# Moving first-table tiles, adaLN units and unsplit products between the stages of a two-layer step

## The chip, the cores and the metric

One core of a Trainium2 chip runs the whole step as one program. The time is device microseconds from the start to the end of one execution, the median of several; smaller is better. PE (TensorE) does the matmuls and PEld its weight loads, DVE (VectorE) and ACT (ScalarE) work on elements, POOL (GpSimd) issues the gathers, SP and ACT issue the plain DMAs.

## What is computed

Two layers, each over 128 prompt tokens and 512 latent tokens of width 1024. A layer has an adaLN part (shift, scale and gate vectors, a product of a condition with `w_ada`), four mixer branches, an output product, and at the end the expert part, which is what the change touches:

```
def peer(u, lp):                       # xt: 512 latent tokens x 1024
    q = (xt @ lp['w_peer_q']).reshape(t, 8, 2, 128)
    sc = einsum('thpc,hpkc->thpk', q, lp['peer_keys'])     # 8 heads, 2 halves, 128 keys
    v1, i1 = top_k(sc[:, :, 0], 16); v2, i2 = top_k(sc[:, :, 1], 16)
    cand = v1[..., :, None] + v2[..., None, :]
    cidx = i1[..., :, None] * 128 + i2[..., None, :]
    top, pos = top_k(cand, 16)
    idx = take_along_axis(cidx, pos); w = softmax(top)
    act = gelu(einsum('td,tkd->tk', xb, tab_u[ib]))        # 16384 experts of width 1024
    out = einsum('tk,tkd->td', wb * act, tab_v[ib])
```

The adaLN part is `m = silu(cond) @ w_ada + b_ada`, cut into six vectors; the second layer norm of a layer uses two of them, and the residual after the experts uses the gate `g2`.

## The kernel before, in words

The prompt tokens run as a generator of small steps (`hook` takes a few at a time at a low priority, by rates that differ from stage to stage); the latent tokens are the main line. Of the 512 latent tokens one block of 128 fetches its expert rows one by one (`gather`, L1207: indirect DMAs on POOL, dot products and sums on DVE). The other three blocks, 384 tokens, are taken densely against all 16384 experts, 128 tiles of 128 experts. A framework orders the instructions of each engine when the program is built: what is ready in its own model of time and stands first in the source goes first. The engines then run their lists in order.

A float32 product is made in one of two ways. *Split*: `load_unit` (L338) loads 512 KB, ACT casts it to a high part (`whi`), DVE subtracts to get a low part (`wlo`), and PE makes three products for each of 8 blocks, 24 matmuls. *Unsplit*: `load_raw` (L333) alone, and PE makes 8 float32 products (16 instructions in the trace). The pool `wp` holds three raw tiles and three pairs of parts.

The expert part of a layer goes through these stages:

- `ln_mod` (L488) makes the normalized, modulated tokens `u` (two parts) and `raw` (one float32 tile in the buffer `big`), and the first two of the 16 query products.
- *The selection*, `peer_top` (L1079): for each of the 16 half heads a query product (`gemm_T`, L346, split, or `gemm_raw`, L358, unsplit where `g % 4 < PQF[l]`), and scores against the keys (L1087). After the second half of a head come `select` (DVE: top 16 of each half, of the candidates, and the indices) and `AQ[l]` adaLN units. One unit (`ada_unit`, L405) loads 2 x 512 KB and makes 8 small matmuls and a few more.
- *Early tiles*, `s_early` (L1250): layer 1 only, `NEA = (0, 4)`. Four tiles of the first table are made unsplit from `raw`, and their gelu is written to DRAM (`gsp`); they are tiles 6, 36, 66 and 96.
- *The weight build*, `wdense` (L1120): the selected weights become a dense matrix W, 12 groups of 32 tokens. DVE and ACT make one-hot tiles, PE multiplies them (L1172), ACT copies 2 MB for each group, and SP writes them to DRAM (`wst`). After each group come `AW[l]` adaLN units.
- *The start*: the adaLN units that are left, a transpose for the gather, and tiles 0 to 5 of the first table (`s_stage`, L1267, split: 24 matmuls, a gelu, kept in `gel`, which has 8 buffers; all use one bank of PSUM, `psS`).
- *The loop*: for each of 128 tiles the columns of W are read back (every fourth tile, `big<-wst`), tile j+6 of the first table is made or, if stored, read (`s_load`), the gelu of tile j is multiplied by W (`v_stage`, L1279) and tile j of the second table is multiplied into the sums (`v_mm`, L1289: 18 matmuls, line 1292). Rows of the gather and steps of the prompt run beside it.

In layer 0 the queue of adaLN units holds 24 when the selection begins (20 for layer 1, 4 for the last gate of layer 0): 8 are called for in the selection, 12 in the weight build, 4 after it. In layer 1 it holds 4, called for in the first groups of the weight build.

Of the kernel before, what the change touches and what calls it, by code (L numbers as in the profile page):

```python
# [8 lines left out]
F32 = mybir.dt.float32  # L9
# [36 lines left out]
GLAG = (6, 1)  # L46
PLAG = (4, 2)
PGL = 0
PQF = (0, 2)
SCB = 6  # L50
LND = 2
NLN = (0, 0)
NPP = 1
WPAD = 128
FILL = (2, 6)
AQ = (1, 0)
AW = (1, 1)
NEA = (0, 4)
LT = 3
NAO = (1, 1)  # L60
AUTO = 2
# [172 lines left out]
def build(tc, A, O, layers=L, tap=None, stop=None):  # L234
# [35 lines left out]
    def P2(name="p2"):  # L270
        return pss.tile([128, 1024], F32, name=name, tag="s")
# [61 lines left out]
    def load_raw(src, op=None):  # L333
        raw = (op or wp).tile([128, 1024], F32, name="wraw", tag="wraw", bufs=8 if op else None)
        nc.sync.dma_start(raw, src)
        return raw
# [110 lines left out]
    def ada_step(n=1, rp=None):  # L447
        for _ in range(max(min(n, len(pend) - hold[0]), 0)):
            ada_unit(*pend.pop(0), rp)
# [626 lines left out]
        V.reciprocal(sm, sm)  # L1076
        tt(out, ex, sm[:, :, None].to_broadcast([128, n, 16]), ALU.mult)

    def peer_top(l, u, pre, raw, scg, idx, wsel, tp):  # L1079
        tops = tp.tile([128, ND, 8, 16], F32, name="topsd", tag="topsd")  # L1080
        with tc.tile_pool(name=f"pq{l}", bufs=2) as qp:
            scs = []

            def score(hd, p, qc, ky):
                pk = P1()
                for b in range(NS):
                    PE.matmul(pk[:, b * 128:(b + 1) * 128], qc[:, b * 128:(b + 1) * 128], ky, start=True, stop=True)  # L1087
                sc = qp.tile([128, ND, 128], F32, name="sc", tag="sc", bufs=SCB)
                S.copy(sc.rearrange("p a b -> p (a b)"), pk[:, 128:T])
                S.copy(scg[:, p, hd], pk[:, 0:128])  # L1090
                scs.append(sc)
                if p:
                    s2 = scs[-2:]
                    for _ in select(tp, ND, lambda p: (lambda b: s2[p][:, b]), idx[:, :, hd], tops[:, :, hd]):
                        pass
                    ada_step(AQ[l])

            last = None
            for g in range(16):
                ky = qp.tile([128, 128], F32, name="ky", tag="ky", bufs=3)  # L1100
                nc.scalar.dma_start(ky, A["keys"][l, :, g * 128:(g + 1) * 128])
                ps = pre[g] if g < 2 else P1()
                if g < 2:
                    pass
                elif g % 4 < PQF[l]:
                    gemm_raw(ps, A["w_pq"][l, g], raw)
                else:
                    gemm_T(ps, load_unit(A["w_pq"][l, g]), u)
                qc = qp.tile([128, T], F32, name="qc", tag="qc")
                S.copy(qc, ps)  # L1110
                if last:
                    score(*last)
                last = (g // 2, g % 2, qc, ky)
                if g == 1:
                    score(*last)
                    last = None
            score(*last)
        topsoft(tp, wsel.rearrange("p a h k -> p (a h) k"), tops.rearrange("p a h k -> p (a h) k"), ND * 8)

    def wdense(l, idx, wsel, wst, wb):  # L1120
        f = lambda a: a.rearrange("p a b -> p (a b)")
        iotam = wb.tile([128, 128, TI], F16, name="iotam", tag="iotam")
        S.copy(iotam, cst[:, C_IOTA:C_IOTA + 128][:, :, None].to_broadcast([128, 128, TI]))
# [22 lines left out]
        for g in range(TD // TW):  # L1146
# [28 lines left out]
                hook(0.5)  # L1175
            nc.sync.dma_start(wst[:, g, :128 * TW], stg.rearrange("p a b -> p (a b)"))
            ada_step(AW[l])

    def rows_of(src, rows, use, gp, bufs, lags):
        q = []  # L1180
# [66 lines left out]
            for _ in nxt:  # L1247
                pass

    def s_early(l, i, raw, sps, dp):  # L1250
        w = load_raw(A["peer_ut"][l, early(l, i)])
        ps = sps[:, i % 2 * 512:i % 2 * 512 + TD]
        for k in range(KD):
            PE.matmul(ps, w[:, k * 128:(k + 1) * 128], raw[:, k, 128:T], start=(k == 0), stop=(k == KD - 1))
        ge = dp.tile([128, TD], F32, name="gel", tag="gel", bufs=NGEL)
        act(ge, ps, AF.Gelu)
        nc.sync.dma_start(gsp[l][i], ge)

    def early(l, i):
        return NGEL - 2 + i * ((128 - NGEL + 2) // max(NEA[l], 1))  # L1260

    def s_load(l, i, dp):
        ge = dp.tile([128, TD], F32, name="gel", tag="gel", bufs=NGEL)
# [31 lines left out]
    def peer(l, u, pre, raw, acc):  # L1295
# [3 lines left out]
        scg = tp.tile([128, 2, 8, 128], F32, name="scg")  # L1299
        idx = tp.tile([128, ND, 8, 16], I32, name="idx")  # L1300
        wsel = tp.tile([128, ND, 8, 16], F32, name="wsel")
        peer_top(l, u, pre, raw, scg, idx, wsel, tp)
        if NEA[l]:
            sps = P2("psS")
            for i in range(NEA[l]):
                s_early(l, i, raw, sps, dp)
        at = {early(l, i): i for i in range(NEA[l])}
        sps = PP("psS") if NPP > 1 else P1("psS")
        with tc.tile_pool(name=f"wb{l}", bufs=1) as wb:
            wdense(l, idx, wsel, wsts[l], wb)  # L1310
        ada_step(len(pend))
        gp = pool(f"pg{l}", 1, fst)
        sh = big()
# [4 lines left out]
                PE.matmul(pt[:, k * 128:(k + 1) * 128], fp(ublk(u[i], k, 0)), ident, start=(i == 0), stop=(i == 1))  # L1318
        S.copy(xts, pt)
        del pt  # L1320
        gels = {j: s_stage(l, j, u, sps, dp) for j in range(NGEL - 2)}
        rate[:] = R_P[l]
        gen = gather(l, scg, xts, acc, tp, gp)
        outs = []
# [574 lines left out]

    dram = pool("dram", 1, space=bass.MemoryType.DRAM)  # L1900
    wsts = [dram.tile([128, TD // TW, 128 * TW + WPAD], F32, name=f"wst{l}") for l in range(layers)]
    gsp = [[dram.tile([128, TD], F32, name=f"gs{l}_{i}") for i in range(NEA[l])] for l in range(layers)]
    x1ds = [[dram.tile([128, D], F32, name=f"x1d{l}_{b}") for b in range(NS)] for l in range(layers)]
    px1 = [dram.tile([128, D], F32, name=f"px1_{l}") for l in range(layers)]
    xins = [[A["x"][(b + 1) * 128:(b + 2) * 128, :] for b in range(NS)]]
# [48 lines left out]
```

## Time and profile before

| | us |
|---|---|
| median of 3 runs | 4409.49 (4405.4 to 4415.57) |
| the profiled execution | 4427.92 |
| its span, first to last instruction | 4426.0 |
| PE busy | 4162.7 |
| DVE busy | 3470.6 |
| ACT busy | 1784.9 |

The profiled execution is one of its own and 18.4 us above the median. Stages of it, in us from the start of the span: layer 0 has its selection from 881 to 1043, its weight build to 1158 and its loop from 1209 on; layer 1 has them from 3071, to 3221, to 3342, and the loop from 3360 to the end. A busy PE is not a PE at its peak: neighbouring matmuls overlap in the records. How long a product takes is therefore read from the chain of waits or from a group's busy time, not from the mean of one matmul.

### The profile page before, as it was taken

What the parts mean: (1) busy time and instruction counts of PE and PEld (TensorE: products, weight loads), DVE (VectorE), ACT (ScalarE), POOL (GpSimd) and SP (SyncE); (2) the same over time, 40 slices, a digit from 0 to 9 for tenths busy, and PEclk for the clock granted to TensorE, in tenths of its full rate; (3) what the DMA queues carried; (4) which work ended last, traced back from release to release, by engine and by line L of the source; (5) the groups of instructions that cost most, each with busy time, mean ns of one, the idle gap of its engine ahead of it and who ended that gap; (6) DMA issues with size and microseconds to landing.
All of it is one profiled execution on the core that took longest, in us unless ns stands there. A gap on an engine that the chain in (4) does not pass through costs nothing.

```text
span 4426.0 us, 63067 instructions
## 1 busy us (share of the span) xinstructions
PE 4162.7 (94%) x22534; PEld 3444.5 (78%) x22534; DVE 3470.6 (78%) x7189; ACT 1784.9 (40%) x3134; POOL 1367.5 (31%) x1028
## 2 busy tenths in 40 slices
PE   8999999787799999999998999998888999999998
PEld 5677677664599999898987667777557889889897
DVE  2236888799998888777777688777999988788887
ACT  3234343347643333433335343433485333333333
POOL 0000443100254444244440044230003554455541
PEclk8999999898899999999999999998989999999999
DMA  6654676537899999899995577473268999999996
GB/s 225 207 189 150 226 236 218 173 126 251 313 358 340 347 337 335 275 359 336 345 342 187 183 243 240 162 240 135 85 238 328 356 346 331 336 334 349 358 333 214
DMA packets 440857, 1182.41 MB, mean 267 GB/s; under 512 B 43056, under 2 KB 153696, under 8 KB 437216
## 3 DMA queue, kind: packets, MB, share of 16 engines
q1 hardware_dynamic: 279600, 625.72, 41.0%
q0 software_dynamic: 147456, 536.94, 34.2%
q10 hardware_dynamic: 13488, 15.75, 1.1%
q8 instruction: 177, 2.90, 0.3%
q14 instruction: 136, 1.11, 0.1%
HBM read 1116.05 MB, written 62.19 MB: 266 GB/s over the span
## 4 chain that ended last, share of the span: by engine, by line
PE 72%; DVE 12%; DMA 8%; issue 4%; ACT 3%; POOL 1%; ACTq 0%; SPq 0%; POOLq 0%; DVEq 0%
PE psS L1273 22%; PE pout L1292 21%; PE p L352 9%; PE pp L1446 5%; DVE eq L246 1%; POOL row L1188 1%; PE pss L646 1%; DVE wlo L246 1%; DMA wraw<-in_peer_v_dram 1%; PE pss L641 1%; PE psw L1172 1%; PE p L681 1%; PE psada L420 1%; DMA row<-in_peer_u_dram,pidx 1%; PE p L511 1%
## 5 line engine op out<-in xcount | busy, mean ns | idle before, releaser
L341 ACT CAST whi<-wraw 128x1024 fp32r<-128x1024 f32 x662 | 694.5, 1050 | 1024.1 <-PE psS L1273 645.1
L246 DVE TENSOR_TENSOR wlo<-wraw,whi 128x1024 fp32r<-128x1024 f32 x662 | 806.8, 1220 | 360.2 <-ACT whi L341 357.8
L1273 PE MATMUL psS<-u,whi 128*128 128x384 f32 x4032 | 1052.5, 342 | 33.6 <-ACT gel L243 27.8
L1273 PEld LDWEIGHTS psS<-u,whi 128*128 128x128 f32 x4032 | 742.1, 190 | 61.8 <-ACT gel L243 34.1
L1273 PE MATMUL psS<-u,wlo 128*128 128x384 f32 x2016 | 687.4, 341 | 4.9 <-DVE wlo L246 4.9
L1188 POOL DMA_INDIRECT row<-in_peer_u_dram,pidx x256 | 317.5, 1240 | 1187.2 <-ACT pidx L1067 460.8
L352 PE MATMUL p<-u,whi 128*128 128x512 f32 (+1 forms) x1760 | 596.0, 414 | 5.6 <-ACT whi L341 5.2
L1188 POOL DMA_INDIRECT row<-in_peer_u_dram,idg x256 | 359.7, 1405 | 616.2 <-DVE dots L1199 383.8
L1188 POOL DMA_INDIRECT row<-in_peer_v_dram,idg x256 | 363.8, 1421 | 533.7 <-DVE accs L1205 446.2
L1188 POOL DMA_INDIRECT row<-in_peer_v_dram,pidx x256 | 326.3, 1275 | 654.8 <-DVE pacc L1205 283.1
L1292 PE MATMUL pout<-wlo,ph 128*128 128x512 f32 x1536 | 502.1, 402 | 0.0
L1292 PE MATMUL pout<-whi,ph 128*128 128x512 f32 x1536 | 500.5, 401 | 1.0 <-ACT whi L341 1.0
L1292 PE MATMUL pout<-whi,pl 128*128 128x512 f32 x1536 | 500.1, 401 | 0.0
L352 PEld LDWEIGHTS p<-u,whi 128*128 128x128 f32 (+1 forms) x1760 | 328.9, 191 | 89.6 <-issue 10.6
L1273 PEld LDWEIGHTS psS<-u,wlo 128*128 128x128 f32 x2016 | 383.0, 190 | 6.0 <-DVE wlo L246 5.7
L352 PE MATMUL p<-u,wlo 128*128 128x512 f32 (+1 forms) x880 | 362.2, 412 | 19.3 <-DVE wlo L246 19.1
L1205 DVE SCALAR_TENSOR_TENSOR pacc<-row,pdots,pacc 128x1024 f32<-128x1024 f32 x254 | 324.8, 1279 | 35.7 <-PE p L352 25.9
L1199 DVE CUSTOM_DVE_ANT_0 row<-row,pu 128x1024 f32<-128x1024 f32 x256 | 310.4, 1218 | 49.8 <-DMA row<-in_peer_u_dram,pidx 26.1
L1284 ACT CAST ph<-gel 128x384 fp32r<-128x384 f32 x256 | 131.3, 513 | 528.1 <-PE pout L1292 510.5
L1292 PEld LDWEIGHTS pout<-whi,pl 128*128 128x128 f32 x1536 | 287.6, 188 | 64.5 <-issue 0.8
L1292 PEld LDWEIGHTS pout<-wlo,ph 128*128 128x128 f32 x1536 | 287.0, 188 | 62.8 <-issue 0.6
L1205 DVE SCALAR_TENSOR_TENSOR accs<-row,ge,accs 128x1024 f32<-128x1024 f32 x254 | 325.7, 1282 | 5.6
(494 smaller groups left out, 6564.0 us busy)
## 6 DMA issues: line engine op xcount, KB each, us to landing
wraw<-in_peer_ut_dram SPq DMA_DIRECT2D x256, 512.0 KB
wraw<-in_peer_v_dram SPq DMA_DIRECT2D x256, 512.0 KB
wraw<-in_w_ada_dram SPq DMA_DIRECT2D x96, 512.0 KB
wraw<-in_w_in_dram SPq DMA_DIRECT2D x96, 512.0 KB
pw<-in_w_in_dram SPq DMA_DIRECT2D x192, 256.0 KB
big<-wst SPq DMA_DIRECT2D x64, 768.0 KB
wst<-stg SPq DMA_DIRECT2D x12, 2048.0 KB
wst<-big SPq DMA_DIRECT2D x12, 2048.0 KB
```

Of the source, the lines that this page charges most:

```text
L246: V.tensor_tensor(out=out, in0=a, in1=b, op=op)
L341: S.copy(hi, raw)
L352: i = PE.matmul(ps[:m, :T], a[:, o:o + m], b[:, k], start=(n == 0), stop=(n == 3 * KD - 1))
L420: PE.matmul(ps[32 * k:32 * k + 32, :256], c32[:, 4 * hf + k, :], w[:, k * 256:(k + 1) * 256], start=(hf == 0), stop=(hf == 1 and not (isg ...
L511: i = PE.matmul(p, a[:, k * 128:(k + 1) * 128], b[:, k], start=(k + n == 0), stop=(k == KD - 1 and n == 2))
L1188: pace(G.indirect_dma_start(out=t, out_offset=None, in_=A[src], in_offset=bass.IndirectOffsetOnAxis(ap=ix, axis=0)), lags[0])
L1199: return V.tensor_tensor_reduce(out=t, in0=t, in1=x, scale=1.0, scalar=0.0, op0=ALU.mult, op1=ALU.add, accum_out=dst)
L1205: return V.scalar_tensor_tensor(out=acc, in0=t, scalar=ge, in1=acc, op0=ALU.mult, op1=ALU.add)
L1273: PE.matmul(ps, a[:, k * 128:(k + 1) * 128], b[:, k, 128:T], start=(n == 0), stop=(n == 3 * KD - 1))
L1284: S.copy(ph, ge)
L1292: PE.matmul(outs[d][hf], a[:, d * 128:(d + 1) * 128], b[:, hf * 512:(hf + 1) * 512], start=(j == 0 and i == 0), stop=(j == 127 and i == le ...
L1446: i = PE.matmul(ps[:m, :128], w[k // 4][:, o:o + m], u[:, k], start=(k == 0), stop=(k == KD - 1))
```

## The change

- `s_early` is replaced by `s_raw` and a generator `raw_tiles`. Both layers make 6 unsplit tiles (`NRAW = (6, 6)`; tiles 6, 26, 46, 66, 86 and 106), one after the `select` of each head from the second on, instead of none in layer 0 and four after the selection in layer 1. They use a bank of the pool of single banks.
- `split_tiles` yields once after each group of the weight build: nothing six times, then tiles 0 to 5 of the first table, one after each of the last six groups. Before, they came after the build. `NSPL` is (0, 0), so no split tile is stored.
- `PQF` goes from (0, 2) to (2, 2): in layer 0 six of the 14 query products of the selection become unsplit, as they are in layer 1.
- adaLN units: `NLN` goes from (0, 0) to (4, 4), four units ahead of `ln_mod`; `AQ` from (1, 0) to (0, 0), none in the selection; `AW` from (1, 1) to (2, 1), two after each group of layer 0's build.

```diff
--- before.py
+++ after.py
@@ -46,16 +46,17 @@
 GLAG = (6, 1)
 PLAG = (4, 2)
 PGL = 0
-PQF = (0, 2)
+PQF = (2, 2)
 SCB = 6
 LND = 2
-NLN = (0, 0)
+NLN = (4, 4)
 NPP = 1
 WPAD = 128
 FILL = (2, 6)
-AQ = (1, 0)
-AW = (1, 1)
-NEA = (0, 4)
+AQ = (0, 0)
+AW = (2, 1)
+NRAW = (6, 6)
+NSPL = (0, 0)
 LT = 3
 NAO = (1, 1)
 AUTO = 2
@@ -1076,7 +1077,7 @@
         V.reciprocal(sm, sm)
         tt(out, ex, sm[:, :, None].to_broadcast([128, n, 16]), ALU.mult)
 
-    def peer_top(l, u, pre, raw, scg, idx, wsel, tp):
+    def peer_top(l, u, pre, raw, scg, idx, wsel, tp, early):
         tops = tp.tile([128, ND, 8, 16], F32, name="topsd", tag="topsd")
         with tc.tile_pool(name=f"pq{l}", bufs=2) as qp:
             scs = []
@@ -1094,6 +1095,8 @@
                     for _ in select(tp, ND, lambda p: (lambda b: s2[p][:, b]), idx[:, :, hd], tops[:, :, hd]):
                         pass
                     ada_step(AQ[l])
+                    if hd:
+                        next(early, None)
 
             last = None
             for g in range(16):
@@ -1117,7 +1120,7 @@
             score(*last)
         topsoft(tp, wsel.rearrange("p a h k -> p (a h) k"), tops.rearrange("p a h k -> p (a h) k"), ND * 8)
 
-    def wdense(l, idx, wsel, wst, wb):
+    def wdense(l, idx, wsel, wst, wb, early):
         f = lambda a: a.rearrange("p a b -> p (a b)")
         iotam = wb.tile([128, 128, TI], F16, name="iotam", tag="iotam")
         S.copy(iotam, cst[:, C_IOTA:C_IOTA + 128][:, :, None].to_broadcast([128, 128, TI]))
@@ -1175,6 +1178,7 @@
                 hook(0.5)
             nc.sync.dma_start(wst[:, g, :128 * TW], stg.rearrange("p a b -> p (a b)"))
             ada_step(AW[l])
+            next(early, None)
 
     def rows_of(src, rows, use, gp, bufs, lags):
         q = []
@@ -1247,17 +1251,34 @@
             for _ in nxt:
                 pass
 
-    def s_early(l, i, raw, sps, dp):
-        w = load_raw(A["peer_ut"][l, early(l, i)])
-        ps = sps[:, i % 2 * 512:i % 2 * 512 + TD]
+    def early_at(l):
+        n = NRAW[l] + NSPL[l]
+        return [NGEL - 2 + i * ((128 - NGEL + 2) // n) for i in range(n)]
+
+    def s_raw(l, j, raw, dp):
+        w = load_raw(A["peer_ut"][l, j])
+        ps = P1("psS")[:, :TD]
         for k in range(KD):
             PE.matmul(ps, w[:, k * 128:(k + 1) * 128], raw[:, k, 128:T], start=(k == 0), stop=(k == KD - 1))
         ge = dp.tile([128, TD], F32, name="gel", tag="gel", bufs=NGEL)
         act(ge, ps, AF.Gelu)
-        nc.sync.dma_start(gsp[l][i], ge)
-
-    def early(l, i):
-        return NGEL - 2 + i * ((128 - NGEL + 2) // max(NEA[l], 1))
+        return ge
+
+    def raw_tiles(l, raw, dp):
+        for i in range(NRAW[l]):
+            nc.sync.dma_start(gsp[l][i], s_raw(l, early_at(l)[i], raw, dp))
+            yield
+
+    def split_tiles(l, u, sps, dp, gels):
+        n = TD // TW - NSPL[l] - (NGEL - 2)
+        for _ in range(n):
+            yield
+        for i in range(NRAW[l], NRAW[l] + NSPL[l]):
+            nc.sync.dma_start(gsp[l][i], s_stage(l, early_at(l)[i], u, sps, dp))
+            yield
+        for j in range(NGEL - 2):
+            gels[j] = s_stage(l, j, u, sps, dp)
+            yield
 
     def s_load(l, i, dp):
         ge = dp.tile([128, TD], F32, name="gel", tag="gel", bufs=NGEL)
@@ -1299,15 +1320,18 @@
         scg = tp.tile([128, 2, 8, 128], F32, name="scg")
         idx = tp.tile([128, ND, 8, 16], I32, name="idx")
         wsel = tp.tile([128, ND, 8, 16], F32, name="wsel")
-        peer_top(l, u, pre, raw, scg, idx, wsel, tp)
-        if NEA[l]:
-            sps = P2("psS")
-            for i in range(NEA[l]):
-                s_early(l, i, raw, sps, dp)
-        at = {early(l, i): i for i in range(NEA[l])}
-        sps = PP("psS") if NPP > 1 else P1("psS")
+        it = raw_tiles(l, raw, dp)
+        peer_top(l, u, pre, raw, scg, idx, wsel, tp, it)
+        for _ in it:
+            pass
+        at = {j: i for i, j in enumerate(early_at(l))}
+        sps = P1("psS")
+        gels = {}
+        it = split_tiles(l, u, sps, dp, gels)
         with tc.tile_pool(name=f"wb{l}", bufs=1) as wb:
-            wdense(l, idx, wsel, wsts[l], wb)
+            wdense(l, idx, wsel, wsts[l], wb, it)
+        for _ in it:
+            pass
         ada_step(len(pend))
         gp = pool(f"pg{l}", 1, fst)
         sh = big()
@@ -1318,7 +1342,6 @@
                 PE.matmul(pt[:, k * 128:(k + 1) * 128], fp(ublk(u[i], k, 0)), ident, start=(i == 0), stop=(i == 1))
         S.copy(xts, pt)
         del pt
-        gels = {j: s_stage(l, j, u, sps, dp) for j in range(NGEL - 2)}
         rate[:] = R_P[l]
         gen = gather(l, scg, xts, acc, tp, gp)
         outs = []
@@ -1899,7 +1922,7 @@
 
     dram = pool("dram", 1, space=bass.MemoryType.DRAM)
     wsts = [dram.tile([128, TD // TW, 128 * TW + WPAD], F32, name=f"wst{l}") for l in range(layers)]
-    gsp = [[dram.tile([128, TD], F32, name=f"gs{l}_{i}") for i in range(NEA[l])] for l in range(layers)]
+    gsp = [[dram.tile([128, TD], F32, name=f"gs{l}_{i}") for i in range(NRAW[l] + NSPL[l])] for l in range(layers)]
     x1ds = [[dram.tile([128, D], F32, name=f"x1d{l}_{b}") for b in range(NS)] for l in range(layers)]
     px1 = [dram.tile([128, D], F32, name=f"px1_{l}") for l in range(layers)]
     xins = [[A["x"][(b + 1) * 128:(b + 2) * 128, :] for b in range(NS)]]
```

## Rows read from the trace of the kernel before

**Rows 1.** The page, part 1: busy us, share of the span, instructions of each engine.

```profile
PE 4162.7 (94%) x22534; PEld 3444.5 (78%) x22534; DVE 3470.6 (78%) x7189; ACT 1784.9 (40%) x3134; POOL 1367.5 (31%) x1028
```

**Rows 2.** Windows: stretch, its us, busy us and instructions of PE, PEld, DVE, ACT, POOL, clock, DMA.

```profile
820.00:881.00 61.00, 46.59 (x311) 42.02 (x310) 44.20 (x100) 31.40 (x45) 0.00 (x0) 0.86 0.35 118
881.00:1043.00 162.00, 135.79 (x741) 97.00 (x741) 151.01 (x808) 70.77 (x154) 5.24 (x3) 0.87 0.44 142
1043.00:1158.00 115.00, 97.08 (x989) 61.81 (x988) 107.83 (x240) 106.83 (x254) 0.00 (x0) 0.95 0.76 285
1158.00:1210.00 52.00, 31.81 (x153) 28.00 (x152) 46.63 (x148) 19.03 (x28) 20.34 (x18) 0.80 0.96 348
3016.00:3071.00 55.00, 40.77 (x269) 36.41 (x269) 40.91 (x96) 29.09 (x44) 0.00 (x0) 0.84 0.34 115
3071.00:3221.00 150.00, 134.04 (x530) 85.22 (x530) 147.64 (x828) 62.10 (x139) 3.81 (x3) 0.93 0.31 96
3221.00:3342.00 121.00, 101.96 (x931) 76.69 (x930) 111.91 (x227) 111.88 (x256) 0.00 (x0) 0.86 0.61 237
```

**Rows 3.** Chain that ended last, layer 0 selection, layer 1 mixers: start us, us, what.

```profile
929.83 12.83 PE p L352 x44
942.66 0.91 PE p L1087 x8
...
2936.20 5.62 PE p L352 x24
```

**Rows 4.** Groups of PE instructions in 3071:3184: name, shape, count, busy us, mean ns.

```profile
L361 PE MATMUL p<-big,wraw 128*128 128x512 f32 x96 | 42.2, 592 | 0.0
```

**Rows 5.** The same chain where the two weight builds begin.

```profile
1016.21 3.68 DMA wraw<-in_w_ada_dram
...
1043.49 2.17 PE psw L1172 x32
...
3205.38 5.43 PE psS L1254 x16
...
3212.66 6.38 DMA wraw<-in_w_ada_dram
...
3220.98 3.41 PE psw L1172 x32
```

**Rows 6.** Timeline of ACT, layer 1: the cast that ends the last selection.

```profile
3205.60 0.23 ACT L1067 CAST idx<-fi 128x48 int32<-128x48 int16 x1 [0.28 <-DVE fi L246]
```

**Rows 7.** The page, costliest groups: the cast of one 512 KB unit on ACT.

```profile
L341 ACT CAST whi<-wraw 128x1024 fp32r<-128x1024 f32 x662 | 694.5, 1050 | 1024.1 <-PE psS L1273 645.1
```

**Rows 8.** The tile gel: ns of one (min/median/max), first and last start.

```profile
L243 ACT ACTIVATE gel<-psS x256: 470/484/494, 1181.3 to 4379.6; 128x384 f32<-128x384 f32 x128
```

**Rows 9.** Groups of instructions in 1043:1181: the copy of an adaLN unit.

```profile
L425 ACT COPY m<-psada 128x256 f32<-128x256 f32 x11 | 3.9, 356 | 0.7 <-PE psada L420 0.7
```

**Rows 10.** Timeline of the SP queue: the last piece of W written, both layers.

```profile
1157.70 0.35 SPq L1176 DMA_DIRECT2D wst<-big  x1
...
3342.30 0.33 SPq L1176 DMA_DIRECT2D wst<-big  x1
```

**Rows 11.** Timeline of PE: the first product of the second table, both layers.

```profile
1209.21 0.73 PE L1292 MATMUL pout<-whi,ph 128*128 128x512 f32 x2 [0.96 <-ACT whi L341]
...
3360.42 0.64 PE L1292 MATMUL pout<-whi,ph 128*128 128x512 f32 x2
```

**Rows 12.** Windows of line 1273 alone: busy us and matmuls of PE and PEld.

```profile
1043.00:1210.00 167.00, 27.70 (x122) 25.77 (x123) 0.90 0.82 305
3221.00:3360.00 139.00, 39.10 (x156) 29.54 (x157) 0.86 0.63 239
```

**Rows 13.** Windows of all engines early in the loop of layer 1.

```profile
3460.00:3521.00 61.00, 56.51 (x274) 50.47 (x273) 55.77 (x111) 22.48 (x31) 34.01 (x25) 0.97 0.97 348
```

**Rows 14.** The chain in the loop of layer 1, where a stored tile is read.

```profile
3612.36 4.24 PE psS L1273 x24
3616.60 8.40 PE pout L1292 x36
```

## The prediction

> **What bounds the kernel now.** I read the share of busy time first: PE is busy for 94% of the span [rows 1], but that is an average over stages with different limits, and the change touches the stages where PE is not the limit. So the next view is the table of windows, stage by stage. In the selections DVE is nearly full (151 of 162 us and 148 of 150 us), PE has gaps, and the transfers are light, 0.44 and 0.31 of their time [rows 2]. In the weight builds DVE and ACT are both full (108 and 107 of 115 us in layer 0), and PE is busy for 97. At the start of layer 0's loop, from 1158 to 1210, PE is busy for 32 of 52 us at a granted clock of 0.80. In the loop PE is the limit and the transfers are close behind it (share 0.97) [rows 13].
>
> The third view is the chain of waits, for the price of a product and for what ends last where a stage hands over. A split product of 512 columns takes 5.62 us of the chain, the scores of one half head 0.91 [rows 3]; six unsplit products took 42.2 us, 7.03 each [rows 4]; an unsplit tile of the first table takes 5.43 [rows 5], a split one 4.24 [rows 14]. So unsplit work is dearer on PE and saves one cast of 1.05 us on ACT [rows 7] and one subtraction on DVE.
>
> **The selection.** Removed from layer 0: eight adaLN units and six casts with their subtractions. Added: six unsplit tiles, and 6 x (7.03 - 5.62) = 8.5 us for the query products that become unsplit. In both layers PE then has 16 x 0.91 + 8 x 5.62 + 6 x 7.03 + 6 x 5.43 = 14.6 + 45.0 + 42.2 + 32.6 = 134.4 us to do before the last scores are out. DVE needs 16.8 us a head: in layer 1 it went from 3071 to the cast that ends the selection at 3205.6 [rows 6], eight heads. Eight heads are 134.4 us too, but the last head can only begin when its scores are there, so the ends add: 134.4 + 16.8 = 151.2 us. From there to the first product of the build took 3221.0 - 3205.6 = 15.4 us in layer 1, of which 6.4 was an adaLN load that stood ahead of it in PE's list [rows 5]; that load is gone, 9.0 stay. With 2 us for the adaLN units ahead of the norm, the first product of the build comes at 881 + 151.2 + 9.0 + 2 = 1043 in layer 0, where it was 1043.5: no change, since the removed waits for adaLN loads (3.7 us for one [rows 5]) pay for the tiles. In layer 1 it comes at 3233 where it was 3221: **+12 us**. There the four early tiles stood beside DVE's last head and cost little; six tiles between the heads push the last scores back. Ends: if the tiles hide under DVE, -17 and -4; if the SP queue, which must write each gelu to DRAM and holds the next weight loads behind that write, makes PE wait, +8 and +18.
>
> **adaLN units ahead of the norm.** No row shows them there. PE was busy for 47 of 61 us and 41 of 55, the transfers for 0.35 and 0.34 [rows 2], so 8 loads of 512 KB find room. I take 2 us a layer (included above), between -3 (PE idles less, and the clock there was 0.86 and 0.84) and +8 (the loads of the first query products stand behind them on SP, and DVE's list waits for their casts).
>
> **The weight build of layer 0.** It gains six tiles, each a cast of 1.05 and a gelu of 0.48 us on ACT [rows 7, 8], together 9.2, and eight adaLN units of one or two copies of 0.36 us [rows 9], about 5. ACT goes from 106.8 to 121 us; at the same filling (0.93) the build takes 130 us. Transfers: 12 pieces of W of 2.1 MB, 40 adaLN loads and 6 of tiles of 0.524 MB are 49.3 MB; 285 GB/s at a share of 0.76 [rows 2] would be 375 at a full one, and 131 us. Both say **+15 us**. Ends: +6, which is layer 1's build of 121 us, and +30, if writes and loads don't fill each other's gaps. Layer 1's build loses four adaLN units and gains about one tile: 0.
>
> The Trainium skill, "DMA: Bandwidth & Descriptors", Specifications, puts the limit of HBM for one core at about 358 GB/s. The loop's 348 at a share of 0.97 [rows 13] agrees with it, the 375 from the build is above it. By it the build would take 138 us, and the sum 4371.
>
> **The start of the loop.** In layer 0 the first product of the second table came 51.5 us after the last piece of W went out [rows 10, 11], with 122 / 24 = 5.1 tiles of the first table done [rows 12]. Layer 1 shows what is left when the tiles are made earlier: the framework already pulls them into the build there, and the same distance is 18.1 us, the time to write the last piece, read it back and multiply, with 156 / 24 = 6.5 tiles done and one more read from DRAM. After the change layer 0 has tiles 0 to 5 from the build, 6 from DRAM and 7 made in those 18 us. The gain is 51.5 - 18.1 + 2.9 x 4.24 = **-46 us**. The four adaLN units and PE's idle time there are in the 51.5. In layer 1 half a tile, **-2 us**. What is late next is the second table's load and the gather: early in layer 1's loop PE idled for 4.5 of 61 us [rows 13]; I charge **+5** (0 to +10) to layer 0, which will begin as abruptly. POOL's list doesn't change.
>
> **The loop.** Each stored tile saves 24 matmuls. In layer 1 the chain shows two second-table tiles back to back there (8.40 us, 36 matmuls) and no wait behind them [rows 14], so the 4.24 us are won whole. Tile 6 is counted in the start; layer 0 wins five, **-21 us**, layer 1 has five where it had three, **-8.5 us**.
>
> **The sum.** Layer 0: 0 + 15 - 46 + 5 - 21 = -47. Layer 1: 12 + 0 - 2 - 8.5 = +1.5. Together -45.5: the profiled execution of 4427.9 us becomes 4382, and against the median, 18.4 us lower, 4364. With each term's ends the forecast's own range is 4340 to 4400.
>
> **Rivals.** *The tiles hide in the selections.* If the framework places them only where PE waits for DVE, both selections stay at DVE's 134.4 us: -17 and -4 in place of 0 and +12, so 4364 - 33 = 4331. For it: DVE is the fullest engine there. Against: PE's own sum is just as long. A rule leads the same way: the Trainium skill, "Perfetto Trace Analysis", Optimization Strategy, says that where the most-contended engine changes, interleaving the regimes may help; no run here shows this pair interleaved.
>
> *Slower: the build waits for adaLN loads.* Place: PE's list in layer 0's build, where 20 units with two loads each now stand among the one-hot products, and their loads stand behind 2 MB writes in the SP queue. PE runs in order; one unit whose load is late holds up the products, then ACT and DVE, which wait for the one-hot buffers. Price: a load cost PE 3.7 to 6.4 us where units were crowded [rows 5]. At 5 us a unit that is 100 us, less 18 of PE's idle time in the build and less the 15 already counted: +67, or 4431. It decides against the change from 3.9 us a unit. Against it: twelve units in the same stage filled the transfers to 0.76 only.
>
> *The loop gives nothing back.* With the transfers at 0.97 [rows 13] the saved matmuls could turn into waits for rows and tables: -21 and -8.5 become 0 and the start's +5 becomes +10, 4364 + 34.5 = 4398. Against: rows 14.
>
> **How the numbers follow.** Forecast 0.50, hidden tiles 0.20, slower 0.17, loop gives nothing 0.13. The measurement tells about 0.2%, 9 us, from no change: 4401 to 4418 is "same". Faster: 0.47 + 0.20 + 0.06 = 0.73; same: 0.03 + 0.02 + 0.07 = 0.12; slower 0.15. The range 4325 to 4425 leaves out the lower part of the hidden-tile case and most of the slower one.
>
> **What would show it.** First product of the build near 1043 and near 3230; PE nearly without gaps in both selections. Layer 0's build 125 to 140 us. From its last write to the first product of the second table some 18 us. In both loops 36 second-table matmuls in a row where tiles 26 to 106 are read. Wrong if psada waits for DMA fill the build, if the selections end with DVE full and PE idle, or if waits for the second table's loads follow each stored tile.

## The result, and the profile after

The changed kernel took 4443.4 us in the median of 12 runs (4428.4 to 4472.1), the kernel before 4416.3 beside it (4405.4 to 4425.1). The ratio is 1.0067, 95% interval 1.0048 to 1.0087: **slower by 0.7%, 27 us between the medians**, where I had forecast 4364 and put the upper end at 4425. The profiled run of after spans 4440.9 us, 14.9 more than the one of before; since that one was 12 us above its median, the traces can place about half of the loss.

First the table of windows, in the columns of [rows 2], cut at after's own stages (norm, selection, build, start; first layer 0, then layer 1):

```profile
820.00:881.00 61.00, 54.31 (x373) 43.30 (x372) 46.05 (x115) 31.56 (x53) 0.00 (x0) 0.92 0.55 183
881.00:1039.00 158.00, 148.67 (x630) 92.49 (x630) 140.07 (x770) 62.64 (x139) 2.81 (x3) 0.92 0.39 123
1039.00:1174.00 135.00, 115.56 (x1147) 78.59 (x1146) 125.04 (x324) 117.01 (x272) 0.94 (x1) 0.96 0.78 289
1174.00:1195.00 21.00, 15.44 (x66) 14.15 (x65) 20.35 (x90) 13.51 (x19) 0.18 (x1) 0.84 0.84 289
3017.00:3075.00 58.00, 52.17 (x338) 37.18 (x336) 40.56 (x95) 30.06 (x52) 0.00 (x0) 0.88 0.54 178
3075.00:3238.00 163.00, 153.24 (x614) 107.04 (x614) 149.11 (x788) 69.10 (x144) 3.13 (x3) 0.98 0.33 103
3238.00:3356.00 118.00, 94.02 (x835) 73.29 (x836) 111.56 (x245) 109.32 (x249) 0.00 (x0) 0.77 0.49 203
3356.00:3373.00 17.00, 12.37 (x64) 11.92 (x64) 17.00 (x83) 9.37 (x14) 0.00 (x0) 0.80 0.98 336
```

PE is now the fuller engine in both selections (148.7 of 158 us, 153.2 of 163), layer 0's build takes 135 us where it took 114, and its start 21 where it took 51.5. So these stages went nearly as forecast, and layer 0's loop begins 14 us earlier [rows 11]. The SP queue (start, us, queue, line, what) and the first product of the second table in layer 0:

```profile
1173.68 0.43 SPq L1179 DMA_DIRECT2D wst<-big  x1
L1313 PE MATMUL pout<-whi,ph x2: 394/396/398, 1195.1 to 1195.3; 128*128 128x512 f32 x2
```

The loops are where it is lost. Windows from the first to the last product of the second table, layer 0 and layer 1; first of before:

```profile
1209.20:2376.80 1167.60, 1162.54 (x6105) 1044.04 (x6106) 944.51 (x1300) 430.86 (x641) 509.17 (x378) 1.00 0.93 332
3360.40:4407.80 1047.40, 1035.24 (x5124) 927.17 (x5122) 884.87 (x1177) 374.00 (x510) 506.83 (x370) 1.00 0.94 336
```

and of after:

```profile
1195.00:2380.40 1185.40, 1145.71 (x5940) 1021.94 (x5939) 945.15 (x1279) 418.95 (x625) 548.02 (x393) 0.98 0.93 332
3373.00:4422.60 1049.60, 1025.48 (x5043) 915.66 (x5042) 883.66 (x1196) 368.74 (x506) 517.24 (x370) 0.99 0.93 334
```

PE has less to do (165 and 81 matmuls fewer), and yet layer 0's loop takes 18 us longer and layer 1's 2 us. PE idles for 40 us of the first where it idled for 5. The last column hardly moves: 332 and 332, 336 and 334 GB/s. And layer 0's loop now issues 393 gather rows, not 378: before had issued 15 of them during its slow start, ahead of the loop. Fifteen rows of 0.524 MB are 7.9 MB, an estimated 24 us at 332 GB/s.

What PE waits for is in the waits of these stretches (us in all, times, longest). Layer 0's loop of before:

```profile
ACT whi L341 <- DMA wraw<-in_peer_v_dram: 20.3, 5, 4.5
PE psS L1273 <- ACT gel L243: 3.5, 1, 3.5
```

and of after:

```profile
ACT whi L342 <- DMA wraw<-in_peer_v_dram: 87.3, 14, 11.9
PE psS L1294 <- ACT gel L244: 26.9, 11, 6.9
ACT whi L342 <- DMA wraw<-in_peer_ut_dram: 12.8, 12, 3.3
```

A load of the second table is late, ACT's cast waits for it, the next gelu stands behind that cast in ACT's list, and PE's next first-table tile waits for the one PSUM bank that the gelu must empty. In the chain of after such a load stands in both loops (start us, us, what):

```profile
1333.06 17.63 DMA wraw<-in_peer_v_dram
...
3585.24 16.69 DMA wraw<-in_peer_v_dram
```

Just ahead of most such loads stands DVE's subtraction that frees one of the three raw tiles (at 4057.56, for one, it ends as a load of 15.86 us is issued): a load is late by its own time and by the moment its tile came free. No run changes the number of raw tiles, so these two are not told apart.

Over half of PE's 40 us of idle time lie early in layer 0's loop, three windows of after:

```profile
1210.00:1260.00 50.00, 41.03 (x196) 36.03 (x195) 38.04 (x56) 13.57 (x19) 31.70 (x20) 0.93 0.97 353
1260.00:1310.00 50.00, 43.72 (x214) 37.78 (x212) 44.38 (x65) 13.98 (x19) 33.20 (x23) 1.00 0.98 367
1310.00:1360.00 50.00, 44.34 (x196) 40.59 (x197) 40.99 (x65) 14.78 (x21) 26.93 (x21) 0.86 0.95 353
```

Here the transfers are full and PE is not. The milestones of both traces, in us from the start:

| | before | after |
|---|---|---|
| layer 0: first product of the build / of the second table / last of the loop | 1043 / 1209 / 2377 | 1039 / 1195 / 2380 |
| layer 1: first score / first product of the build | 3071 / 3221 | 3075 / 3238 |
| layer 1: first of the second table / last of the loop | 3360 / 4408 | 3373 / 4423 |

One trace places such points to some 5 us: in the 14 traces of this study layer 0's first score comes between 873 and 885, whichever of the edits a kernel has. In the five kernels below whose layer 1 has the same edits (e4, e9 to e12), its loop takes 1041 to 1048 us. A difference of a few us between two traces says nothing by itself.

### The profile page after: what moved, and what is told of

Its sections match the earlier page's. It is cut to its first block, busy times and chain, and to the rows that moved or that the text cites. A ratio compares the mean times of both kernels' runs of the same rounds, so it can differ in the third digit from the quotient of the medians.

```text
span 4440.9 us, 62863 instructions
## 1 busy us (share of the span) xinstructions
PE 4181.0 (94%) x22422; PEld 3433.0 (77%) x22422; DVE 3458.9 (78%) x7175; ACT 1773.0 (40%) x3123; POOL 1394.3 (31%) x1028
## 4 chain that ended last, share of the span: by engine, by line
PE 63%; DVE 14%; DMA 12%; issue 5%; ACT 4%; POOL 2%; ACTq 0%; DVEq 0%; SPq 0%; POOLq 0%
PE psS L1294 16%; PE pout L1313 16%; PE p L353 9%; PE pp L1469 5%; DMA wraw<-in_peer_v_dram 3%; DVE wlo L247 2%; POOL row L1192 2%; DVE row L1203 2%; PE p L362 2%; DMA row<-in_peer_u_dram,pidx 1%; PE pss L647 1%; PE pss L642 1%; PE p L682 1%; PE p L379 1%; DMA row<-in_peer_v_dram,pidx 1%
## 5 line engine op out<-in xcount | busy, mean ns | idle before, releaser
L342 ACT CAST whi<-wraw 128x1024 fp32r<-128x1024 f32 x648 | 679.5, 1050 | 1054.4 <-PE psS L1294 519.9
L1294 PE MATMUL psS<-u,whi 128*128 128x384 f32 x3904 | 1029.8, 345 | 63.2 <-ACT gel L244 57.9
L247 DVE TENSOR_TENSOR wlo<-wraw,whi 128x1024 fp32r<-128x1024 f32 x648 | 790.5, 1222 | 336.8 <-ACT whi L342 308.4
L1294 PEld LDWEIGHTS psS<-u,whi 128*128 128x128 f32 x3904 | 723.5, 192 | 94.7 <-ACT gel L244 69.7
L1294 PE MATMUL psS<-u,wlo 128*128 128x384 f32 x1952 | 670.2, 343 | 4.6 <-DVE wlo L247 4.5
L353 PE MATMUL p<-u,whi 128*128 128x512 f32 (+1 forms) x1664 | 562.3, 412 | 0.1
L1192 POOL DMA_INDIRECT row<-in_peer_v_dram,pidx x256 | 346.0, 1351 | 662.4 <-PE p L362 176.7
L353 PEld LDWEIGHTS p<-u,whi 128*128 128x128 f32 (+1 forms) x1664 | 309.4, 190 | 78.2 <-issue 10.4
L353 PE MATMUL p<-u,wlo 128*128 128x512 f32 (+1 forms) x832 | 340.2, 409 | 5.8 <-DVE wlo L247 5.8
L1469 PEld LDWEIGHTS pp<-pu,pw 128*128 128x128 f32 x1984 | 280.1, 196 | 62.7 <-DMA pw<-in_w_in_dram 12.9
```

The source lines that it names most:

```text
L247: V.tensor_tensor(out=out, in0=a, in1=b, op=op)
L342: S.copy(hi, raw)
L353: i = PE.matmul(ps[:m, :T], a[:, o:o + m], b[:, k], start=(n == 0), stop=(n == 3 * KD - 1))
L1192: pace(G.indirect_dma_start(out=t, out_offset=None, in_=A[src], in_offset=bass.IndirectOffsetOnAxis(ap=ix, axis=0)), lags[0])
L1294: PE.matmul(ps, a[:, k * 128:(k + 1) * 128], b[:, k, 128:T], start=(n == 0), stop=(n == 3 * KD - 1))
L1469: i = PE.matmul(ps[:m, :128], w[k // 4][:, o:o + m], u[:, k], start=(k == 0), stop=(k == KD - 1))
```

## The experiments

Theory A: in the loops the transfers set the pace, so that saved products turn into waits and an earlier start is given back. Theory B: PE sets the pace there, as forecast, and the loss lies in selections and builds. Theory C: the reads of stored tiles do harm by their place. Ratios are to the kernel before on the same chip, with their 95% interval.

**Stored tiles made again.**

```diff
-gels[n] = s_load(l, at[n], dp) if n in at else s_stage(l, n, u, sps, dp)
+gels[n] = s_stage(l, n, u, sps, dp)
```

> The changed kernel, but its loops read no stored tile: all tiles from 6 on are made in the loop again (the six unsplit ones of the selections are still made and written, and not used). Theory A (the transfers set the pace of the loop, so a tile that is read saves PE time that turns into waits): each tile made again costs its extra bytes alone, 0.524 - 0.197 = 0.33 MB or about 1 us at 345 GB/s, so 12 tiles cost 0 to 12 us: 4443 to 4455, with fewer waits of ACT's cast for second-table loads. Theory B (PE sets the pace of the loop as I forecast, and the loss lies in the selections and builds): 12 x 4.24 = 51 us more, 4494. Theory C (the reads themselves do the harm, by their place among the loads): faster than the changed kernel, 4415 to 4435.

Ratio 1.0066 (1.0050 to 1.0082), as the changed kernel. Its loops:

```profile
1197.50:2383.60 1186.10, 1162.45 (x6083) 1039.97 (x6082) 953.17 (x1285) 427.80 (x636) 531.36 (x393) 0.99 0.93 334
3381.60:4432.00 1050.40, 1041.57 (x5161) 933.73 (x5160) 890.06 (x1198) 376.35 (x515) 510.16 (x370) 1.00 0.93 335
```

PE does 17 and 16 us more and the loops are as long, 1186 and 1050. Twelve tiles read in place of made are worth nothing here. B, which wanted 51 us more, falls for the loops, and C too. ACT's waits for second-table loads, 87.3 and 92.9 us in the loops of after, are shorter here (layer 0, layer 1):

```profile
ACT whi L342 <- DMA wraw<-in_peer_v_dram: 57.3, 13, 11.1
ACT whi L342 <- DMA wraw<-in_peer_v_dram: 48.2, 12, 6.3
```

Where the saved time went can be seen behind each read. Here are the 72 us that follow each of the five reads in a loop, added up: layer 0 of after (reads at 1384, 1547, 1713, 1885, 2104) and the same stretches of this run, 3 us later by its later start; then layer 1 (3532, 3701, 3867, 4037, 4206; 9 us later).

```profile
sum 360.00, PE 345.00 PEld 308.67 DVE 280.13 ACT 114.80 POOL 166.41; mean PE 69.00 PEld 61.73 DVE 56.03 ACT 22.96 POOL 33.28
sum 360.00, PE 360.00 PEld 325.96 DVE 291.52 ACT 121.51 POOL 166.18; mean PE 72.00 PEld 65.19 DVE 58.30 ACT 24.30 POOL 33.24
sum 360.00, PE 342.33 PEld 304.37 DVE 294.99 ACT 123.81 POOL 190.18; mean PE 68.47 PEld 60.87 DVE 59.00 ACT 24.76 POOL 38.04
sum 360.00, PE 358.41 PEld 323.31 DVE 307.05 ACT 128.13 POOL 187.08; mean PE 71.68 PEld 64.66 DVE 61.41 ACT 25.63 POOL 37.42
```

Behind the reads PE idles for 15.0 and 17.7 us; without them, at the same places, for 0 and 1.6. So the saved matmuls became waits within 72 us, which the prediction had named as a sign of being wrong. PE's idle time early in layer 0's loop, 21 us from 1210 to 1500, is the same in both runs and does not come from the reads.

**Half of the gather left out**, in the kernel before and in the changed one:

```diff
-            rows = [(h, k) for h in range(HG) for k in range(16)]
+            rows = [(h, k) for h in range(HG) for k in range(8)]
...
-            while done < 256 * (G_P[l] ...
+            while done < 128 * (G_P[l] ...
```

> The kernel before with half of the dense experts' gather left out (k from 0 to 7 of 16, so part of the sampled tokens' sum over rows is missing), 128 rows of 0.524 MB fewer a layer, about 67 of some 390 MB of a loop, spread over the same tiles. Theory A: PE already set the pace of this loop in its first half (590 of 590 us), so it gains little, 0 to 25 us by shorter waits: 4390 to 4416. It is the base of the next run.

> The changed kernel with the same half of the gather left out. Theory A (transfers set the pace of the changed loop): with a sixth of the loop's bytes gone PE sets the pace again, the start's 14 us, the tiles made ahead and the stored tiles all count, and the changed kernel is 30 to 50 us faster than the kernel before with the same part left out. Theory B (the loss lies in selections and builds, whose transfers this leaves alone): it stays 20 to 30 us slower than that. Between the two, 0 to 15 us faster: both hold in part.

0.9975 (0.9965 to 0.9986) and 0.9912 (0.9898 to 0.9927): with a sixth of the loop's bytes gone, the same change makes the kernel 0.6%, some 28 us, **faster**. Loops of the light kernel before, then of the light changed one:

```profile
1203.00:2364.60 1161.60, 1158.45 (x6073) 1037.10 (x6074) 797.70 (x1094) 424.71 (x635) 345.16 (x251) 1.00 0.81 275
3346.90:4384.20 1037.30, 1032.38 (x5124) 926.44 (x5122) 738.94 (x985) 374.72 (x511) 348.78 (x242) 1.00 0.82 275
```

```profile
1191.30:2346.50 1155.20, 1135.18 (x5907) 1011.31 (x5905) 799.73 (x1082) 413.86 (x620) 362.26 (x265) 0.99 0.83 282
3342.20:4366.60 1024.40, 1019.55 (x5043) 913.36 (x5041) 737.26 (x1002) 370.10 (x505) 353.42 (x242) 1.00 0.82 276
```

Taking rows away from the kernel before is worth 0.25%, 11 us; taking PE's work out of the loops with all rows there was worth nothing; only both together pay. In layer 1 PE is full, and the 81 matmuls fewer (two more stored tiles, and what was made ahead) shorten the loop by 12.9 us, nearly the 14 that they are at 4.24 us for 24. In layer 0 the gain is 6 of some 30, and 20 us of PE's idle time are left; PE is busy for 84 of the first 100 us from 1210, where the transfers are at 0.95 to 0.99 even so. The start of layer 0's loop is its own crowd: that, half the rows don't cure. The gain is just under the 30 to 50 expected.

So the loss lies in the loops and comes from what the gather asks of them, as A says. A row asks two things, though: a transfer, and an operation on DVE, whose busy time in layer 0's loop falls with the rows from 945 to 798 us. The pair alone does not tell these apart; a window of e8, below, speaks for the transfers.

**The parts, one by one.** From the kernel before (units ahead of the norm; then layer 0's query products unsplit; then all units out of the selection) and from the changed one (no unsplit tiles; and of that, query products split again, or the units put back):

```diff
 e4   -NLN = (0, 0)    +NLN = (4, 4)          (before)
 e9   -PQF = (0, 2)    +PQF = (2, 2)          (e4)
 e10  -AQ = (1, 0)     +AQ = (0, 0)           (e9)
      -AW = (1, 1)     +AW = (2, 1)
 e5   -NRAW = (6, 6)   +NRAW = (0, 0)         (after)
 e6   -PQF = (2, 2)    +PQF = (0, 2)          (e5)
 e7   -AQ = (0, 0)     +AQ = (1, 0)           (e5)
      -AW = (2, 1)     +AW = (1, 1)
```

> The kernel before with four adaLN units a layer moved ahead of the second norm, and nothing else of the change. In the changed kernel the norm was done 9.7 us earlier in layer 0 and about 11 earlier in layer 1, counted from the layer's beginning, and I put it down to these units. If that is so and the kernel before passes it on: 10 to 20 us faster, 4396 to 4406. If the time is given back in the loop (theory A, transfers): layer 0's part is lost and layer 1's too, 4410 to 4416. If the earlier norm came from other parts of the change: no norm earlier, 4416 or more.

> The changed kernel without the six unsplit tiles between the heads of the selections (so nothing is written and read back either); the tiles between the groups of the weight build, the moved adaLN units and the unsplit query products stay. Theory A (a stored tile saves PE time that the loop can't use, while it costs the selection 5.2 us of PE on its bounding chain): the selections end 10 to 25 us earlier, the loops hardly need longer: 4400 to 4425, faster than the changed kernel by 20 to 40 us. Theory B (stored tiles are worth their 4.24 us each): 12 x 4.24 = 51 us more in the loops against some 35 won in the selections: 4455 to 4465.

> As the run before, and layer 0's six unsplit query products are split again as in the kernel before. Without the unsplit tiles DVE should bound the selection, so the six casts and six subtractions (1.1 us each on DVE) cost more than the 8.5 us of PE that they save: 0 to 8 us slower than the run before. If PE still bounds it: up to 8 us faster.

> As the first run of this set, but eight adaLN units stand between the heads of layer 0's selection again and one, not two, after each group of the build (four a layer stay ahead of the norm). The build of layer 0 should get shorter by up to 10 us and the selection longer by 4 to 10: -8 to +6 against the first run. If crowded units were the loss of the changed kernel (the slower rival of the prediction), it is 15 us or more faster.

> The kernel before with four adaLN units a layer ahead of the norm and with layer 0's six query products unsplit; no tile of the first table is moved. The pair of runs with and without the unsplit query products differed by 21 us, while PE waited 18 us for the subtractions of the split ones. If the two gains add and the loop keeps them: 4397 - 21 = 4376. If layer 0's loop, whose pace the transfers set, gives most of it back: 4385 to 4400.

> As the run before, and all eight adaLN units taken out from between the heads of layer 0's selection, two after each group of the weight build, as in the changed kernel. It differs from the changed kernel in the tiles of the first table alone: none between the heads, none placed in the build, and layer 1's four after the selection as in the kernel before. In the pair of runs on these units the crowded build cost 9.5 us: 5 to 15 us slower than the run before. If the tiles are the whole loss of the changed kernel, it lies 35 us or more under 4443.

| kernel | ratio | interval | median us |
|---|---|---|---|
| e4: four units a layer ahead of the norm | 0.9943 | 0.9926 to 0.9960 | 4396.8 |
| e9: e4, query products unsplit | 0.9957 | 0.9941 to 0.9973 | 4395.7 |
| e10: e9, units out of the selection | 0.9970 | 0.9955 to 0.9986 | 4409.3 |
| e5: the change without unsplit tiles | 1.0010 | 0.9994 to 1.0026 | 4421.4 |
| the change | 1.0067 | 1.0048 to 1.0087 | 4443.4 |
| e6: e5, query products split again | 1.0052 | 1.0036 to 1.0068 | 4442.3 |
| e7: e5, units back in the selection | 0.9989 | 0.9973 to 1.0005 | 4411.9 |

Down the first five rows each step adds a part of the change. All that isn't a first-table tile makes the kernel 0.3% faster (e10); the tiles cost 0.97%, 43 us: 0.57%, 25 us, for the six unsplit ones a layer, and 0.4%, 18 us, for placing six in each build while layer 1 loses its four stored ones. Those four were worth something: layer 1's loop took 1043 us in e10 and 1061 in e5, more than layer 0's loop won by ending at 2356, not 2367. Over all traces with the whole gather it took 1041 to 1048 us with the four, 1050 to 1063 with none (e1, e5, e6, e7). Why six stored ones gave no more than 1050 is open; means of 336, 334 and 332 GB/s are too near each other to tell. Layer 1's loops of e10 and e5:

```profile
3350.00:4393.00 1043.00, 1031.30 (x5091) 923.74 (x5089) 885.14 (x1190) 371.61 (x507) 510.22 (x369) 0.99 0.94 336
3338.00:4399.00 1061.00, 1045.26 (x5168) 937.49 (x5168) 889.48 (x1195) 375.85 (x513) 511.29 (x371) 0.99 0.93 332
```

Without unsplit tiles layer 0's selection ended 21 us earlier (19 counted from its first score), and DVE bounds it (e5, columns as above):

```profile
881.00:1018.00 137.00, 117.87 (x523) 73.40 (x522) 134.35 (x752) 56.89 (x131) 3.82 (x3) 0.88 0.33 109
```

e4's gain isn't where I had put it: its first score came no earlier in either layer (878 us against 882; 697 us behind layer 0's last product against 694). What went is the four units behind layer 0's build, 4.2 MB of loads, and in layer 1 the four inside it: there the way from the build's first product to the loop's took 134.5 us, not 139.6. The trace is of a run of 4416 us, 19 above e4's median, so it can place only 12 of the 24 us. In layer 0 e4 wrote its last piece of W at 1156.5 and began the second table at 1176, 19 us, with 145 first-table matmuls done by 1181, six tiles: the framework pulls tiles into a build of twelve units by itself. With twenty units there (e10) it does not: last piece at 1145.5, second table at 1199. Yet the two loops end at 2368 and 2367: 23 us of earlier start are worth nothing at the end. Layer 0's loop of e4, of e10 and, below them, of the last run (e12):

```profile
1176.00:2368.20 1192.20, 1166.69 (x6105) 1044.25 (x6106) 965.27 (x1367) 430.24 (x642) 544.15 (x394) 0.99 0.93 331
1199.00:2367.00 1168.00, 1162.57 (x6105) 1043.94 (x6106) 935.90 (x1239) 424.38 (x632) 517.95 (x379) 1.00 0.93 332
```

```profile
1174.00:2356.00 1182.00, 1166.31 (x6105) 1044.83 (x6106) 967.43 (x1369) 431.08 (x643) 535.34 (x394) 0.99 0.94 334
```

The query products were a miss both ways. In e6 PE waited in layer 0's selection for the subtractions of the split ones, and the build began 20 us later than in e5, 12 of them counted from the first score:

```profile
PEld p L353 <- DVE wlo L247: 18.0, 4, 9.4
PE p L353 <- DVE wlo L247: 16.4, 3, 8.8
```

In e9, with units between the heads, the medians with and without them are equal, though in the traces the build begins 8 us earlier and layer 0's loop ends 13 us earlier. As e4's trace is of a run 19 us above its median and e9's of one at its median, this shows no gain. What they are worth there stays unsettled.

**Rows moved.** e8 slows the prompt's rows in the changed kernel's loops; e11 is e10, and e12 is e9, with fewer of layer 0's own gather rows in its first 80 tiles:

```diff
 e8   -R_P = ((1.67, 2.5, 0.5), (0.81, 1, 1.38))
      +R_P = ((1.67, 1.7, 0.4), (0.81, 0.8, 1.1))
 e11, e12   -G_P = (0.35, 0.6)   +G_P = (0.3, 0.6)
```

> The changed kernel with the prompt's gather rows taken at a slower rate in the loops (2.5 to 1.7 and 0.5 to 0.4 a tile in layer 0, 1 to 0.8 and 1.38 to 1.1 in layer 1), so that some of them move to other stages; nothing is left out. Theory A: layer 0's loop, with fewer transfers beside its tables, gets back 10 to 20 us of waits for second-table loads; if the rows left over find room in layer 1's mixers, 4420 to 4435; if they pile up behind layer 1's loop, slower than 4443. Theory B: layer 0's loop takes as long as in the changed kernel (some 1183 us from the first product of the second table to the last).

> As the run before, and layer 0's loop takes 0.30 in place of 0.35 of its 256 gather rows in its first 80 tiles, the rest later; PE's work is the same. Theory A: the first 600 us of that loop, where the transfers are at 0.97 and PE waits for second-table loads, have about 13 rows, 6.7 MB or 19 us of transfers fewer, and the last 400 us have them more, at shares of 0.92 to 0.96: 0 to 10 us faster than the run before. Theory B: no difference in the first part of the loop.

> The kernel before with the four adaLN units a layer ahead of the norm, layer 0's six query products unsplit, and 0.30 in place of 0.35 of layer 0's gather rows in the first 80 tiles of its loop; no tile of the first table is moved. Without the later rows this kernel had 71 us of waits for second-table loads in layer 0's loop and took 1189 us for it. Theory A: the loop is as long as its transfers take, and those in its first part get fewer: 1175 to 1185 us for the loop, 4380 to 4393 in all. Theory B: no change, 4396.

e8 took 1.0456 (1.0433 to 1.0479): the prompt's own products left the loop with its rows (layer 0's took 1086 us, but PE did 104 us less in it), the mixers took 859 us where they took 695, and 123 us of leftovers stood behind the last product. As a kernel it is a miss. Its windows speak for A:

```profile
1260.00:1310.00 50.00, 49.78 (x250) 44.67 (x249) 44.17 (x82) 22.36 (x31) 19.44 (x14) 1.00 0.91 322
1310.00:1800.00 490.00, 490.00 (x2445) 441.05 (x2444) 346.45 (x437) 173.85 (x236) 184.46 (x124) 1.00 0.85 284
1800.00:2260.00 460.00, 428.17 (x2067) 381.20 (x2066) 403.51 (x503) 146.63 (x200) 283.64 (x202) 0.96 0.98 366
```

At 284 GB/s PE has no gap for 490 us, although three stored tiles are read there (1364, 1528, 1692); where the rows bunch, at 366, it has 32 us of them. The first of these windows also stands above for after. DVE is as busy in both, 44.2 and 44.4 of 50 us, while the transfers are at 322 GB/s here and at 367 there, and PE is busy for 49.8 and 43.7 us. In that one window the transfers differ and DVE's work does not; no run has that for the whole loop.

e11 took 0.9957 (0.9940 to 0.9974) and 4400.9 us, 8 under e10; its waits for second-table loads in layer 0's loop fell from 22.9 to 11.6 us. e12 took 0.9930 (0.9911 to 0.9949), 4386.3 us: **57 us under the changed kernel and 30 under the one before, the fastest that leaves nothing out**, with layer 0's loop at 1182 us, e9's having taken 1189. Both went as A expects, though in each pair the intervals of the two kernels overlap.

## Why the prediction was wrong

**Right.** The build of layer 0 begins at 1039 (forecast 1043), 163 us behind the first score, where it was 162. Layer 1's selection is longer by 13 us from its first score to the build (150 to 163; forecast +12), and PE sets it: in the chain of after unsplit tiles stand among query products and scores without a gap.

```profile
3096.06 0.89 PE p L1088 x8
3096.95 5.16 PE psS L1262 x16
3102.11 6.87 PE p L362 x16
3108.98 0.89 PE p L1088 x8
3109.87 5.62 PE p L353 x24
3115.49 0.89 PE p L1088 x8
3116.38 5.16 PE psS L1262 x16
```

The price of 5.43 us a tile was 5.16. So the rival of hidden tiles was wrong. The Trainium skill, "Perfetto Trace Analysis", Optimization Strategy, says that interleaving regimes may help where the most-contended engine changes; the pair is interleaved here, and PE then took the place of DVE as the bound.

The units ahead of the norm were put at +2 us a layer; no such delay shows. The crowded build took 134.5 us from first product to last write (forecast 130), so the slower rival with its 5 us a unit was not the cause either; e7 puts units and selection together at 0.2%. The start took 21.4 us (forecast 18.1), with 6.0 tiles made and one read (forecast 8).

**Wrong: what the loops make of it.** Three terms rest on one assumption, that the loop's PE time is its length: "the 4.24 us are won whole" (-21 and -8.5), the 2.9 tiles ahead in the start's -46 (-12), and the +5 for the early loop. Together they put layer 0's loop at -28 us and layer 1's at -8.5. The traces have +18 and +2: 57 of the 61 us by which the profiled run of after, 4443.2, lies above the 4382 forecast for it.

In layer 0 PE saved 17 us of busy time, its idle time grew from 5 to 40 us, and the loop took 18 us more. (The 165 matmuls fewer are 29 us at 4.24 for 24; the granted clock was 0.98, not 1.00.) The tiles made again part the two causes. With PE as busy as in before, 1162 us, that loop is 18.5 us longer than before's: this is the early start, so the +5 and the -12 were +18.5 together. Reading the tiles then takes 17 us from PE's busy time and adds 16 to its idle time: -21 was -1. In layer 1 PE saved 10 us, idled 12 more, and the loop took 2 more: -8.5 was nothing.

The evidence that misled me were rows 14: two products in a row without a wait at one stored tile of four. They show that a buffer had been filled ahead at that place, not that the transfers could keep it filled. At the next stored tile of the same loop, whose two products begin at 3864, a second-table load stood in the chain 12 us behind them:

```profile
3884.89 12.29 DMA wraw<-in_peer_v_dram
```

[rows 13] spoke against me too: I read PE as the limit there, but PE idled for 4.5 of these 61 us while the transfers were at 0.97. Over the whole loop of before both limits lay on each other: PE was busy for 1163 of 1168 us while 388 MB went at 332 GB/s. In this loop neither limit alone gave back much time: less PE work gave none, half the gather 11 us in all.

The rival that was right, "the loop gives nothing back", got 0.13 and the wrong price, 4398. It zeroed the loop's terms and left the start's gain standing. If the bytes set the end, the earlier start is given back too: with layer 0 at nothing (not -21) it is 4420, and the 7 us by which the base of three runs lay low make it 4427. Some 16 us to 4443 are left; in the traces +3.6 of them are layer 0's, and the rest I can't place.

The Trainium skill, "DMA: Bandwidth & Descriptors", Specifications, puts a core's share of HBM at about 358 GB/s, under which the sum was estimated at 4371. The windows of after run from 353 to 367 GB/s where PE idles, so the traces neither keep that figure as a ceiling nor contradict its size.

## What to carry to other kernels

Where an engine is full and the transfers nearly are (0.93 of their time here), price a saved instruction by what it saves on both, and test it with bytes taken away: if the change helps only then, it sits on the wrong limit. Two loops that started 23 us apart ended together here: on that evidence an early start of such a loop is worth only the bytes moved before it starts, so count the transfers that the slow start used to carry. Read a wait at every place where the same thing happens, not at one. Look first for what can leave a crowded place for an idle one: four units moved ahead of a norm were worth 25 us, twelve stored tiles cost that much.

## What the runs showed of the hardware

Some of PE's waits came with a lower granted clock and so cost more than their length: it was 0.93 and 0.86 in two of the three windows of the early loop, with 9 and 6 us of gaps, a mean between the levels of 1.2 and 2.4 GHz (the third had 6 us of gaps and 1.00). In the chain of after, the first-table tile behind the load of 17.63 us at 1333 took 7.05 us where such a tile takes 4.24 [rows 14]:

```profile
1352.27 7.05 PE psS L1294 x24
```

In layer 1's build, with PE busy for 94 of 118 us, the clock was 0.77, and 0.86 before [rows 2], where PE was busy for 102 of 121.
